# One padding tile on the right side of SBUF grows by 128 bytes, so that large matmul operands begin at multiples of 256 bytes

## The chip, the cores and the metric

The kernel runs on one core of a Trainium2 chip. The metric is the device time of one execution in microseconds (us). SBUF, the on-chip memory that TensorE (PE) reads its operands from, is addressed in bytes within each of its 128 partitions. Pools of tiles are laid out from both of its ends: most pools grow upward from the low end ("left"), pools with `side="right"` grow downward from the high end.

## The reference

One layer of a diffusion backbone over 1024 latent tokens with a prefix of 256 context tokens, D = 1024, all in float32:

```python
h_x = rms_norm(x, g_norm1) * (1 + sc1) + sh1                    # and h_c from the context
y_x, _ = token_mixer(h_x, h_c, ...)   # one input projection h @ w_in, then two branches:
    # A: gelu, layer norm, 128x128 mixing of positions per channel group, @ w_branch_a
    # B: gated linear attention in both directions, in chunks of 64 tokens, @ w_branch_b
    # (sigmoid gate * A + sigmoid gate * B) @ w_out
x = x + gt1 * y_x
tokens = rms_norm(x, g_norm2) * (1 + sc2) + sh2
y = moe_ffn(tokens, ...)              # 16 experts, top group, top 2 in it:
    # (silu(t @ w_g[e]) * (t @ w_u[e])) @ w_d[e], weighted by the router
return rms_norm(x + gt2 * y, g_final)
```

## The kernel before

Every large product is made from float32r operands that are split in two, a high part and the rest: `hi` is a copy on ScalarE (ACT) into float32r, `lo` the difference on VectorE (DVE). A product is then the sum of hi·hi, hi·lo and lo·hi. A matmul has a stationary operand, which an LDWEIGHTS (PEld in the profile) puts into the array, and a moving operand of up to 512 columns, which streams through. In a name such as `mm<-zh,wh` the moving operand stands first and the stationary one second.

The stages that matter here, in the order of time, with the two operands of their matmuls:

- To about 360 us: the rows are normalised into `hxh`, `hxl` (left side), and the projections q, v and k are made. `wload` (line 244) brings 1 MB of a weight into `wraw` and `split` (lines 237 and 238) makes `wh`, `wl` of it; all of these lie on the right side, in pool `wp`. `gemm` (line 256) issues the matmuls. With 512 columns `hx` moves and `w` is stationary; with 256 or 264 columns `w` moves and `hx` is stationary.
- 360 to 686 us: the gated linear attention, and between its blocks further projections (`side_tile`) with `hx` moving over 512 columns.
- 686 to 868 us: the spatial gating, first with `w` moving over 256 columns, then with `hx` moving over 512.
- 868 to 955 us: `@ w_branch_a`, with `zh`, `zl` moving (right side, pool `zp`) and `wh`, `wl` stationary.
- 955 to 1045 us: `@ w_branch_b`, with `gbh`, `gbl` moving (left side) and `wh`, `wl` stationary.
- 1045 to 1153 us: `@ w_out` (line 994), 256 columns: stationary is `m` (right side), moving are `wh`, `wl` (right) for half of the columns and `woh`, `wol` (left) for the other half. The router runs along with it.
- From 1160 us: the experts. A page is 1 MB of an expert's weights. It lands in one of ten page tiles on the right side (`praw`, `raw`), ACT and DVE split it into an `hl` tile (`part`, lines 1192 and 1193), and `block_a` (line 1372) streams the `hl` tile in twelve matmuls of 512 columns past `xah`, `xal`, `aah` or `aal` (left side, stationary). Nine of the experts have further rows, which `block_b` (line 1385) takes straight from the page tile over 256 columns.

Three `hl` tiles take turns. The first two of each round lie in pool `mt1` on the right side, the third in pool `ep` on the left:

```python
def split_tile():
    n = used[1] % 3
    used[1] += 1
    return (ep_ if n == 2 else mt1).tile([128, 2, 2048], F32R, name="hl", tag=("m0", "m1", "hl")[n], bufs=1)

def block_a(acc, st, k0, pg, start, stop):
    wh, wl = pg
    for k in range(2):
        for n, (x, w) in enumerate(((0, wh), (0, wl), (1, wh))):
            for h in range(2):
                end = PE.matmul(acc[h], st[x][:, k0 + k, :], w[:, k, 512 * h:512 * h + 512], ...)
```

One page is thus four matmuls on the stationary `xah`, two on `xal`, four on `xah` and two on `xal`. The engines take their instructions in the order of the program; SyncE (SP) issues nearly all loads of weights, and a load waits until its tile is free.

Two padding tiles stand at the start of the memory: `pad_l` of 16 floats in the left pool `cp`, and `pad_r` of 24 floats, the first tile of the first right pool. Nothing reads them.

Of the kernel before, what the change touches and what calls it, by code (L numbers as in the profile page):

```python
# [6 lines left out]
F32 = mybir.dt.float32  # L7
# [154 lines left out]
def body(tc, A, out):  # L162
# [40 lines left out]

    cp.tile([128, 16], F32, name="pad_l")
    rp = tc.alloc_tile_pool(name="rp", bufs=1, side="right")
    rp.tile([128, 24], F32, name="pad_r")

    def bcast(key, r0, n, tile_, eng=None):
        a = A["rows"]
# [1477 lines left out]
```

## Time and profile before

| | |
|---|---|
| median of 3 runs | 2250.44 us (2249.14 to 3596.91) |
| the profiled execution | 2251.51 us |
| its span, first to last instruction | 2249.8 us |
| mean granted TensorE clock | 0.984 |
| PE busy | 2170.6 us, 96% |
| DVE busy | 1415.1 us, 63% |
| ACT busy | 1056.9 us, 47% |
| DMA | 529.63 MB, mean 235 GB/s |

The time of the execution is 1.7 us longer than its span. Busy time of PE is the union of its matmuls, each from its start to a modelled end; matmuls overlap, so a new one starts well before the one before it ends, and the pace of PE is read from the starts.

### The profile page before, as it was taken

The numbers are of one execution on the slowest core, as the hardware profiler recorded it, in microseconds if no ns is written. First come the engines' busy times: TensorE is split into PE (matmuls) and PEld (weight loads), VectorE is DVE, ScalarE is ACT, GpSimd is POOL, SyncE is SP. The second block draws the span as 40 slices with busy tenths as digits, with TensorE's granted clock in tenths as the row PEclk, the third lists the DMA queues.
The fourth block names the chain that finished last, engine by engine and source line by source line (L and its number), as shares of the span: only waits on it lengthen the run. The fifth ranks groups of instructions, "written<-read, shape, count | busy, mean of one in ns | idle before, by whom it ended". The sixth has DMA issues, their size and how long they took to land. (4 is left out here: it accounts for less than half of the span.)

```text
span 2249.8 us, 36046 instructions
## 1 busy us (share of the span) xinstructions
PE 2170.6 (96%) x14286; PEld 1787.4 (79%) x14287; DVE 1415.1 (63%) x2127; ACT 1056.9 (47%) x1327; POOL 213.0 (9%) x174
## 2 busy tenths in 40 slices
PE   8999999999999999999969999999999999999975
PEld 6999898888889978888967777777778777777754
DVE  5744215847672354245888578787878787677666
ACT  3412114634542244233226456665667576555553
POOL 0011000000000000000342110000101010100031
PEclk9999999999999999999989999999999999999987
DMA  7576433556652176445658779797989898877774
GB/s 295 178 228 177 155 130 102 192 172 208 215 187 71 57 260 208 168 149 195 189 189 319 253 274 362 284 369 297 367 291 377 298 351 314 296 274 284 280 245 157
DMA packets 141792, 529.63 MB, mean 235 GB/s; under 512 B 17127, under 2 KB 57759, under 8 KB 94513
## 3 DMA queue, kind: packets, MB, share of 16 engines
q1 hardware_dynamic: 119584, 467.84, 57.1%
q0 software_dynamic: 20880, 55.16, 8.5%
q10 hardware_dynamic: 1152, 4.26, 0.6%
q8 instruction: 114, 1.87, 0.3%
q14 instruction: 62, 0.50, 0.1%
HBM read 457.09 MB, written 70.31 MB: 234 GB/s over the span
## 5 line engine op out<-in xcount | busy, mean ns | idle before, releaser
L1193 DVE TENSOR_TENSOR hl<-praw,hl 128x2048 fp32r<-128x2048 f32 x174 | 400.2, 2302 | 137.3 <-ACT hl L1192 134.1
L1372 PE MATMUL pa<-hl,xah 128*128 128x512 f32 x1536 | 428.1, 399 | 19.8 <-ACT hl L1192 13.2
L1192 ACT ACTIVATE hl<-praw 128x2048 fp32r<-128x2048 f32 x174 | 333.4, 1918 | 157.8 <-PE pa L1372 150.9
L1372 PEld LDWEIGHTS pa<-hl,xah 128*128 128x128 f32 x1536 | 286.9, 189 | 91.4 <-ACT hl L1192 13.7
L1193 DVE TENSOR_TENSOR hl<-raw,hl 128x2048 fp32r<-128x2048 f32 x114 | 260.7, 2290 | 91.0 <-ACT hl L1192 88.2
L1192 ACT ACTIVATE hl<-raw 128x2048 fp32r<-128x2048 f32 x114 | 218.6, 1918 | 104.0 <-PE pa L1372 98.2
L1372 PE MATMUL pa<-hl,xal 128*128 128x512 f32 x768 | 241.8, 396 | 0.0
L1372 PE MATMUL pa<-hl,aah 128*128 128x512 f32 x768 | 214.8, 401 | 6.3 <-DVE hl L1193 5.0
L256 PE MATMUL mm<-wh,hxh 128*128 128x256 f32 (+1 forms) x768 | 218.2, 284 | 0.9 <-DVE vv L285 0.6
L256 PE MATMUL mm<-wl,hxh 128*128 128x256 f32 (+1 forms) x768 | 216.8, 282 | 0.0
L256 PE MATMUL mm<-wh,hxl 128*128 128x256 f32 (+1 forms) x768 | 216.6, 282 | 0.0
L256 PE MATMUL mm<-hxh,wh 128*128 128x512 f32 x448 | 178.4, 398 | 0.0
L256 PE MATMUL mm<-hxh,wl 128*128 128x512 f32 x448 | 178.2, 398 | 0.0
L256 PE MATMUL mm<-hxl,wh 128*128 128x512 f32 x448 | 178.1, 398 | 0.0
L1372 PEld LDWEIGHTS pa<-hl,xal 128*128 128x128 f32 x768 | 145.5, 189 | 34.0
L1372 PEld LDWEIGHTS pa<-hl,aah 128*128 128x128 f32 x768 | 142.7, 190 | 37.3 <-DVE hl L1193 5.5
L256 PEld LDWEIGHTS mm<-wh,hxh 128*128 128x128 f32 x768 | 144.6, 188 | 1.9 <-DVE vv L285 0.8
L238 DVE TENSOR_TENSOR wl<-wraw,wh 128x2048 fp32r<-128x2048 f32 (+1 forms) x36 | 82.7, 2298 | 99.7 <-ACT wh L237 99.6
L256 PEld LDWEIGHTS mm<-wl,hxh 128*128 128x128 f32 x768 | 144.7, 188 | 0.0
L256 PEld LDWEIGHTS mm<-wh,hxl 128*128 128x128 f32 x768 | 144.4, 188 | 0.0
L1372 PE MATMUL pa<-hl,aal 128*128 128x512 f32 x384 | 121.4, 396 | 0.0
L237 ACT ACTIVATE wh<-wraw 128x2048 fp32r<-128x2048 f32 (+1 forms) x36 | 69.1, 1918 | 67.3 <-PE mm L256 67.0
(489 smaller groups left out, 3588.2 us busy)
## 6 DMA issues: line engine op xcount, KB each, us to landing
praw<-in_w_gu_dram SPq DMA_DIRECT2D x116, 1024.0 KB
raw<-in_w_gu_dram SPq DMA_DIRECT2D x76, 1024.0 KB
praw<-in_w_d_dram SPq DMA_DIRECT2D x58, 1024.0 KB
raw<-in_w_d_dram SPq DMA_DIRECT2D x38, 1024.0 KB
wraw<-in_w_in_dram SPq DMA_DIRECT2D x24, 1024.0 KB
wraw<-in_w_mod_dram SPq DMA_DIRECT2D x18, 1024.0 KB
vb<-v_d POOLq DMA_DIRECT2D x16, 1024.0 KB, 6.3
xt<-in_x_dram SPq DMA_DIRECT2D x16, 512.0 KB
```

The lines of the kernel that those rows point to most:

```text
L237: SC.activation(wh[:, :n], raw[:, :n], AF.Copy)
L238: V.tensor_sub(wl[:, :n], raw[:, :n], wh[:, :n].bitcast(F32))
L256: end = PE.matmul(acc, Wst[a](k), Wmv[b](k), start=n == 0, stop=n == tot - 1)
L1192: SC.activation(hl[:, 0, :], raw, AF.Copy)
L1193: V.tensor_sub(hl[:, 1, :], raw, hl[:, 0, :].bitcast(F32))
L1372: end = PE.matmul(acc[h], st[x][:, k0 + k, :], w[:, k, 512 * h:512 * h + 512], start=start and (k, n) == (0, 0), stop=stop and (k, n) == ( ...
```

## The change

`pad_r` has 56 floats instead of 24: 224 bytes per partition instead of 96.

```diff
     cp.tile([128, 16], F32, name="pad_l")
     rp = tc.alloc_tile_pool(name="rp", bufs=1, side="right")
-    rp.tile([128, 24], F32, name="pad_r")
+    rp.tile([128, 56], F32, name="pad_r")
```

All tiles of right-side pools move down by 128 bytes; those of left-side pools stay. The built programs have these start addresses, as their remainder on division by 256 (their phase, from here on):

| tiles | side | before | after |
|---|---|---|---|
| `wraw`, `wh`, `wl`, and the page tiles `praw`, `raw` | right | 128 | 0 |
| `zh`, `zl`; `m`; the first two `hl` of a round | right | 128 | 0 |
| `S`, `la`, `kb`, `qb`, `vb`, `vg`, `ug` | right | 128 | 0 |
| `xt` at the start; `w2` | right | 32; 96 | 160; 224 |
| `hxh`, `hxl`, `hc`, `gbh`, `gbl`, `woh`, `wol` | left | 0 | 0 |
| `xah`, `xal`, `aah`, `aal`, `xbT`, `abT`, the third `hl` | left | 0 | 0 |
| `kt`, `ats`, `qq` of the attention | left | 64 | 64 |
| `kf` (the identity of the transposes) | left | 128 | 128 |

A slice that a matmul takes of these tiles begins a multiple of 512 bytes further on, with three exceptions: the chunks of 264 columns (1056 bytes apart, so that the slices go through all eight phases of 32 bytes), the 32-column slices of `xbT` and `abT` (128 bytes apart), and the slices of `qq`. Modulo 512 the two buffers of `wh` lie at 384 and 128 before, since one is 8448 bytes long.

The instructions stand in the same order on every engine, and there are as many. Seven instructions wait for other semaphores, because a tile that was moved by 128 bytes overlaps other tiles of pools released earlier. On SP, at the start of the attention over latent tokens, where `mk` is a small mask and `kb`, `qb` are the first loads of the attention:

```order
 L595 DMA r_d<-vs 128x256 [waits DMAHW7_49,Activation_49]
 L607 DMA w2m<-in_kg_dram 128x1 [waits DMAHW0_49,PE_49]
-L750 DMA mk<-in_ki_dram 128x128 [waits DMAHW1_49,DMASW1_49,PE_49]
+L750 DMA mk<-in_ki_dram 128x128 [waits DMASW1_49,DMASW0_49,DMAHW1_49,PE_49,Pool_49]
 L775 DMA kb<-kT_d 128x4x128 [waits DMAHW2_49]
 L776 DMA qb<-qT_d 128x4x128 [waits DMAHW3_49]
```

The load of `mk` now also waits for an instruction of GpSimd and a DMA of its queue: those of `fold_router` (lines 546, 554 and 555), whose tile `wra` it now overlaps. The other six are a wait that is dropped (the first splits of `w2` on ACT, two passes of `la`, and the loads of `rb` and `wra`) or one added for a DMA of GpSimd's queue (one split into `m` on ACT, at about 1000 us; the last such DMAs before it load `vb` in the attention).

## Rows read from the trace of the kernel before

**Rows 1.** The page's first part: busy us (share of the span) and instructions.

```profile
PE 2170.6 (96%) x14286; PEld 1787.4 (79%) x14287; DVE 1415.1 (63%) x2127; ACT 1056.9 (47%) x1327; POOL 213.0 (9%) x174
```

**Rows 2.** What PE waited for: us in total, times, longest us.

```profile
PE pa L1372 <- ACT hl L1192: 14.5, 2, 13.2
PE pa L1372 <- DVE hl L1193: 10.6, 6, 5.0
```

**Rows 3.** Windows in the `zh` and `gbh` stages: PE busy (matmuls), PEclk, DMA, GB/s.

```profile
870.00:950.00 80.00, 80.00 (x355) 1.00 0.62 214
960.00:1040.00 80.00, 80.00 (x345) 1.00 0.46 145
```

**Rows 4.** `zh` and `gbh`: duration ns min/median/max (modelled ends), first and last start.

```profile
L256 PE MATMUL mm<-zh,wh x128: 389/389/395, 868.6 to 955.0; 128*128 128x512 f32 x128
L256 PE MATMUL mm<-gbh,wh x128: 392/394/398, 955.7 to 1044.5; 128*128 128x512 f32 x128
```

**Rows 5.** Timeline of PE where `hx` moves: start us, us, engine, line, operation.

```profile
779.62 0.39 PE L256 MATMUL mm<-hxh,wl 128*128 128x512 f32 x1
...
781.94 0.39 PE L256 MATMUL mm<-hxh,wh 128*128 128x512 f32 x1
```

**Rows 6.** Timeline of PE in the experts: the first matmuls of consecutive pages.

```profile
1691.20 1.08 PE L1372 MATMUL pa<-hl,aah 128*128 128x512 f32 x4
...
1693.93 1.09 PE L1372 MATMUL pa<-hl,xah 128*128 128x512 f32 x4
...
1696.72 1.10 PE L1372 MATMUL pa<-hl,xah 128*128 128x512 f32 x4
...
1699.53 1.08 PE L1372 MATMUL pa<-hl,xah 128*128 128x512 f32 x4
...
1702.26 0.62 PE L1372 MATMUL pa<-hl,xah 128*128 128x512 f32 x2
```

**Rows 7.** The same earlier: the first matmuls of two consecutive pages.

```profile
1511.61 1.09 PE L1372 MATMUL pa<-hl,xah 128*128 128x512 f32 x4
...
1514.38 0.40 PE L1372 MATMUL pa<-hl,xah 128*128 128x512 f32 x1
```

**Rows 8.** ACT's splits of pages alone: how many began before 1691 us.

```profile
1160.00:1691.00 531.00, 278.05 (x145) 0.98 0.83 307
```

**Rows 9.** Timeline of ACT: splits, idle time before them, what ended it.

```profile
1691.40 1.92 ACT L1192 ACTIVATE hl<-raw 128x2048 fp32r<-128x2048 f32 x1 [0.88 <-PE pa L1372]
1694.13 1.92 ACT L1192 ACTIVATE hl<-praw 128x2048 fp32r<-128x2048 f32 x1 [0.81 <-PE pa L1372]
```

**Rows 10.** Groups of matmuls, shapes apart: count, busy us, mean ns (modelled ends).

```profile
L256 PE MATMUL mm<-hxh,wh 128*128 128x512 f32 x448 | 178.4, 398 | 0.0
L256 PE MATMUL mm<-wh,hxh 128*128 128x256 f32 x512 | 144.7, 283 | 0.0
L994 PE MATMUL mm<-woh,m 128*128 128x256 f32 x256 | 49.2, 286 | 0.0
L994 PE MATMUL mm<-wh,m 128*128 128x256 f32 x256 | 49.2, 285 | 0.0
L697 PE MATMUL s<-vb,kt 128*128 128x256 f32 x192 | 31.1, 292 | 0.3
L697 PE MATMUL s<-ctx_v,kt 128*128 128x256 f32 x48 | 7.8, 292 | 0.0
```

**Rows 11.** What SP's page loads waited for: us in total, times, longest.

```profile
SPq L1179 <- DVE hl L1193: 636.9, 198, 21.3
```

**Rows 12.** Splits, 1400 to 2000 us: count, busy us, mean ns, idle before.

```profile
L1193 DVE TENSOR_TENSOR hl<-praw,hl 128x2048 fp32r<-128x2048 f32 x103 | 235.9, 2292 | 82.6 <-ACT hl L1192 80.4 <-DMA praw<-in_w_gu_dram 0.5
L1192 ACT ACTIVATE hl<-praw 128x2048 fp32r<-128x2048 f32 x103 | 197.7, 1919 | 93.6 <-PE pa L1372 93.6
```

**Rows 13.** `fold_router`'s last DMA and the load of `mk`: duration ns, start us.

```profile
L555 POOL DMA_DIRECT2D wr_d<-br x1: 543/543/543, 317.0 to 317.0; - x1
L750 SPq DMA_DIRECT2D mk<-in_ki_dram x1: 394/394/394, 362.4 to 362.4; - x1
```

## Prediction

> **What bounds the kernel now.** I read the page's first part, then what PE waited for, then the pace of PE's matmuls stage by stage, and last the queues that feed it. PE is busy for 96% of the span [rows 1], and its longest waits for the splits are 14.5 and 10.6 us in all, most of it in one wait of 13.2 us [rows 2]. The time is therefore the number of matmuls times the step from one start to the next, and a change that moves no instruction can pay only if it moves that step.
>
> The step differs between stages that do the same thing. In 80 us of the `zh` stage 355 matmuls lie, in 80 us of the `gbh` stage 345 [rows 3]. About two of either number only reach into the window from before, since a record of 389 or 394 ns [rows 4] is longer than a step; so the steps are 80 / 353 = 226.6 ns and 80 / 343 = 233.2 ns. Shape (512 columns), stationary operands (`wh`, `wl`) and granted clock (1.00, the 2.4 GHz level) are the same, and the faster window has the more DMA traffic (0.62 against 0.46). What differs is where the moving operand begins: `zh` in the phase of `wh` (128 and 128), `gbh` not (0 and 128). `hx` over 512 columns is also in another phase than `wh`: ten steps take 781.94 - 779.62 = 2.32 us, 232 ns each [rows 5].
>
> The experts repeat this inside one stage, over one set of stationary tiles in phase 0. Pages begin at 1691.20, 1693.93, 1696.72, 1699.53 and 1702.26 us, so they last 2.73, 2.79, 2.81 and 2.73 us: a short one in each round of three [rows 6]. Which tile that is follows from the splits. 145 of them began before 1691 us [rows 8], so the one at 1691.40 is the 146th and the one at 1694.13 the 147th, the third of its round, into the left `hl`; it starts 0.2 us after PE has left the page that began at 1691.20 [rows 6, 9], which was thus the left tile's. The tile in phase 0 is the fast one here; in the `zh` stage it was phase 128 on both sides. So what counts, as far as these rows go, is that the moving and the stationary operand begin in the same phase. Region is no rival: the first two `hl` lie within the memory that `zh` had. Nor does a distance of 256 bytes hurt: one of the two `wh` buffers is 256 off `zh` modulo 512, the other 0, and the records of `zh` against `wh` lie between 389 and 395 ns, half of them at 389 [rows 4].
>
> **The change part by part.** It costs no instruction. It brings every large pair into phase 0. Right with right (`zh` and `wh`, `m` and `wh`) was equal and stays equal. The terms:
>
> - `gbh`, `gbl`: three products of 128 matmuls [rows 4] are 384, each from 233.2 to 226.6 ns: 384 x 6.6 = 2.5 us.
> - `hx` over 512 columns: 3 groups of 448 [rows 10] and the 96 of q at the start (8 slices, 4 outputs, 3 products), 1440 in all, from 232 to 226.6 ns: 1440 x 5.4 = 7.8 us. None of PE's longest waits is in these stretches, so all of it lies on the path. Upper end, by the `gbh` difference of 6.6: 9.5 us.
> - Experts: 16 experts of 18 pages are 288, of which 192 lie in the right tiles. They go from 2.80 (the mean of 2.79 and 2.81) to 2.73 us by the rows above. Rounding and another row make this less: a left page on `xah` lasted 1514.38 - 1511.61 = 2.77 us [rows 7]. I take 0.065 us, since 0.07 is also what twelve matmuls at 5.4 to 6.6 ns give (0.065 to 0.079): 192 x 0.065 = 12.5 us. Ends: 0.02 us a page (3.8 us) and 0.079 (15.2 us), with 2 us more if the left pages lose their 2.77 as well (half of 96 by 0.04).
> - Matmuls of 256 columns whose operands come into the same phase: 1536 with `w` moving over `hx`, 288 with `hx` or `hc` moving, 384 with `wo` moving over `m`, together 2208. Their mean is 283 ns where phases differ (`wh,hxh`) and 285 where they are the same (`wh,m`); but `woh,m`, which differs too and lies beside the latter, has 286 [rows 10]. So at 256 columns nothing is gained, and from -1 to +2.3 ns is possible; I take +1: 2.2 us lost, between 2.2 gained and 5.1 lost.
> - The 264-column chunks go through all eight phases before and after: 0. The same holds for `block_b`, whose stationary slices alternate between phases 0 and 128, so that the pairs that match and those that don't change places: 0.
> - The attention's `vb` against `kt` goes from a distance of 64 to one of 192. `ctx_v` against `kt` has 192 already, and both show 292 ns [rows 10]: 0. `ats` has the phase of `kt`: 0.
> - ACT and DVE read and write the moved tiles as well. Their splits into right and left tiles share means of 1919 and 2292 ns, and ACT had 93.6 us of idle time before 103 of them [rows 12], which covers some ns each: 0. The page loads end at another phase too, and they wait for tiles anyway [rows 11]: 0.
> - The wait that `mk` gains: `fold_router`'s last DMA was issued at 317.0, the load of `mk` at 362.4 us [rows 13]. Queued behind it on SP are `kb` and `qb`, for which the attention would wait; with 45 us between them the price is 0. The other six edits wait for less or for what has long landed: 0.
>
> Sum: 2.5 + 7.8 + 12.5 - 2.2 = 20.6 us. Against the profiled execution's own 2251.5 us this is 2230.9; against the median of the runs, 2250.4, it is 2229.8. I predict **2230 us**. With the low ends (2.5 + 7.8 + 3.8 - 5.1 = 9.0) it is 2242, with the high ones (2.5 + 9.5 + 17.2 + 2.2 = 31.4) 2220.
>
> Is PE still what is late in the experts? SP's loads of pages waited 636.9 us for tiles to come free [rows 11], so loads run ahead of PE. DVE needs 2.29 us for a page, ACT 1.92 [rows 12]; split, split and page are 1.92 + 2.29 + 2.73 = 6.94 us, and three tiles turn round in 3 x 2.73 = 8.19. Cover remains, 1.2 us a round; if it went, a page would wait for its split.
>
> The Trainium skill speaks against this change: "SBUF — State Buffer", section "Who interferes with whom", gives TensorE two independent read ports, one for the moving operand and one for the weights, and says that it never waits on anyone. By that the phases of two operands can't matter, and the sum would be 0. The trace disagrees: 226.6 against 233.2 ns.
>
> **The rivals.**
>
> *The experts' gain is lost to supply.* A shorter page asks for weights at 1 MB in 2.73 us, and pages wait for DMA, ACT or DVE instead. For it: the DMA share was 0.83 from 1160 to 1691 us, with 307 GB/s [rows 8], and the 1.2 us of cover hold only while ACT and DVE do nothing else. Against it: the loads wait for tiles, not the reverse [rows 11], and ACT's idle time before splits ended with PE [rows 12]. Only the other terms remain: 2251.5 - 2.5 - 7.8 + 2.2 = 2243.
>
> *No gain.* The step is set by something that goes with the stage and the tile but not with phase, or PE's two streams don't meet. For it: no row shows a pair of 0 and 0 with `w` stationary. Against it: the three-page rhythm inside one stage. 2251 us. The page of the Trainium skill named above would have this case.
>
> *Slower.* At 256 columns the weight load of the next matmul has half the time to hide, and equal phases make it collide: 2.3 ns on each of 2208, 5.1 us, mostly in the projections with `w` moving. This decides the sign once the 512-column terms together are under 5.1 us: with none of them 2251.5 + 5.1 = 2257. For it only 285 against 283 ns; against it `woh,m` at 286.
>
> *More than forecast.* Other pairs (the float32 matmuls of the attention, whose phases no row separates) gain as well: below 2220.
>
> **How the numbers follow.** My forecast has a chance of 0.71, the loss to supply 0.12, no gain 0.10, slower 0.03, more than forecast 0.04. The range must take in the forecast's ends, 2220 and 2242, and the loss to supply at 2243: 2220 to 2244, which leaves out 0.17. A measurement of this kernel can tell about 2% from no change, here 45 us. Faster than 2205 would take twice my sum: 0.03. Slower than 2295 has no mechanism with such a price: 0.01. The rest, 0.96, lies within 2%, most of it faster.
>
> **What would show it.** In the profile after, 80 us of the `gbh` stage should hold 355 matmuls, not 345, and the `gbh` and `hxh` groups of 512 columns a mean of 389 ns, as `zh` has. All A-only pages should last about 2.73 us, with no rhythm of three. The groups of 256 columns should stay within 2 ns, and PE's waits for `hl` should not grow beyond the 25 us of now. I am wrong if the `zh` stage slows down (then phase 128 itself was the fast one), if the rhythm of three is still there (then it was the tile, not its phase), or if pages speed up and the span does not (then supply is late).

## The result

| | before | after |
|---|---|---|
| median | 2250.71 us (6 runs, 2249.14 to 3596.91) | 2234.06 us (6 runs, 2232.93 to 2237.04) |
| ratio, with its 95% interval | | 0.9919 [0.9906, 0.9933] |
| profiled execution; its span | 2251.51; 2249.8 us | 2234.38; 2232.6 us |

The run of 3596.91 us was disturbed and is in no comparison. The forecast was 2230 us with a range of 2220 to 2244: the sign and the range hold, and the gain is 17.2 us of span where the sum said 20.6.

The page's first part after: PE has lost 18.6 us of its busy time [rows 1], the other engines nothing.

```profile
PE 2152.0 (96%) x14286; PEld 1788.1 (80%) x14287; DVE 1414.7 (63%) x2127; ACT 1057.8 (47%) x1327; POOL 212.6 (10%) x174
```

What PE waited for, after (us in total, times, longest): the waits for the splits are what they were [rows 2], 25.4 us against 25.1.

```profile
PE pa L1372 <- ACT hl L1192: 14.9, 2, 13.4
PE pa L1372 <- DVE hl L1193: 10.5, 7, 5.0
```

Windows after (PE busy, matmuls, PEclk, DMA share, GB/s): the first lies where `w` moves over 256 columns, the second in the `zh`, the third in the `gbh` stage.

```profile
690.00:760.00 70.00, 70.00 (x586) 1.00 0.16 53
870.00:950.00 80.00, 80.00 (x355) 1.00 0.62 214
960.00:1040.00 80.00, 80.00 (x355) 1.00 0.48 153
```

The `gbh` window has come from 345 to the 355 of the `zh` window, which has not moved [rows 3]. At 256 columns it has gone the other way: the same window of the kernel before held some more.

```profile
690.00:760.00 70.00, 70.00 (x592) 1.00 0.16 54
```

Tiles after (duration ns min/median/max, first and last start): the `gbh` records now read as those of `zh` [rows 4].

```profile
L256 PE MATMUL mm<-zh,wh x128: 389/389/389, 867.1 to 953.5; 128*128 128x512 f32 x128
L256 PE MATMUL mm<-gbh,wh x128: 389/389/389, 954.2 to 1040.5; 128*128 128x512 f32 x128
L256 PE MATMUL mm<-gbh,wl x128: 389/389/389, 954.6 to 1041.0; 128*128 128x512 f32 x128
L1372 PE MATMUL pa<-hl,xah x1536: 387/389/794, 1177.0 to 2188.5; 128*128 128x512 f32 x192
L1372 PE MATMUL pa<-hl,aal x384: 387/389/628, 1215.8 to 2214.6; 128*128 128x512 f32 x192
```

The same three groups before, for their first and last starts:

```profile
L256 PE MATMUL mm<-gbh,wl x128: 392/395/398, 956.1 to 1045.0; 128*128 128x512 f32 x128
L1372 PE MATMUL pa<-hl,xah x1536: 387/393/792, 1180.8 to 2205.7; 128*128 128x512 f32 x192
L1372 PE MATMUL pa<-hl,aal x384: 387/392/628, 1219.6 to 2231.8; 128*128 128x512 f32 x192
```

With the first starts of `gbh`, 955.7 before [rows 4] and 954.2 after, these give the account of the span. Ahead of `gbh` 1.5 us came; the `gbh` stage went from 89.3 to 86.8 us, 2.5; `w_out` and the router from 135.8 to 136.0, -0.2; the experts from 1051.0 to 1037.6, 13.4. The tail is 18.0 us in both. Together 17.2 us.

Timeline of PE in the experts after: three times a page's twelve matmuls, the last of them ahead of a transpose, take 2.72, 2.72 and 2.73 us. The rhythm of three [rows 6] is gone.

```profile
1689.70 1.07 PE L1372 MATMUL pa<-hl,xah 128*128 128x512 f32 x4
...
1692.42 1.07 PE L1372 MATMUL pa<-hl,xah 128*128 128x512 f32 x4
...
1695.14 1.07 PE L1372 MATMUL pa<-hl,xah 128*128 128x512 f32 x4
...
1697.87 0.60 PE L1562 MATMUL aat<-kf,sa 128*128 128x128 f32 x4
```

Timeline of PE after where `hx` moves in a short run between the attention's small matmuls (the first two rows below bound nine steps: 2.08 us) and in a long run (the last two bound ten: 2.26 us, before 2.32 [rows 5]).

```profile
433.29 0.39 PE L256 MATMUL mm<-hxl,wh 128*128 128x512 f32 x1
...
435.37 0.39 PE L256 MATMUL mm<-hxl,wh 128*128 128x512 f32 x1
...
778.24 0.39 PE L256 MATMUL mm<-hxh,wl 128*128 128x512 f32 x1
...
780.50 0.39 PE L256 MATMUL mm<-hxh,wh 128*128 128x512 f32 x1
```

The same short run before took 2.10 us, so 226 ns a step were reached in the long run, 231 in the short one, where it had been 233:

```profile
433.63 0.39 PE L256 MATMUL mm<-hxl,wh 128*128 128x512 f32 x1
...
435.73 0.40 PE L256 MATMUL mm<-hxl,wh 128*128 128x512 f32 x1
```

Groups after (count, busy us, mean ns), answering to [rows 10]:

```profile
L256 PE MATMUL mm<-hxh,wh 128*128 128x512 f32 x448 | 176.4, 394 | 0.0
L256 PE MATMUL mm<-wh,hxh 128*128 128x256 f32 x512 | 145.5, 284 | 0.0
L994 PE MATMUL mm<-woh,m 128*128 128x256 f32 x256 | 49.5, 288 | 0.0
L697 PE MATMUL s<-vb,kt 128*128 128x256 f32 x192 | 31.2, 292 | 0.3 <-DVE at L678 0.2 <-ACT la L632 0.2
```

`hxh` stops at 394 ns, half way to the 389 that I had named as its sign; the groups of 256 columns keep within the 2 ns that I gave them. `vb` against `kt`, moved from a distance of 64 to 192, shows its 292 ns as before.

### The profile page after: what moved, and what is told of

Same layout as the page of the kernel before. It is cut to its first block, busy times and chain, and to the rows that moved or that the text cites. A ratio compares the mean times of both kernels' runs of the same rounds, so it can differ in the third digit from the quotient of the medians.

```text
span 2232.6 us, 36046 instructions
## 1 busy us (share of the span) xinstructions
PE 2152.0 (96%) x14286; PEld 1788.1 (80%) x14287; DVE 1414.7 (63%) x2127; ACT 1057.8 (47%) x1327; POOL 212.6 (10%) x174
## 5 line engine op out<-in xcount | busy, mean ns | idle before, releaser
L1372 PE MATMUL pa<-hl,xah 128*128 128x512 f32 x1536 | 421.1, 395 | 19.8 <-ACT hl L1192 13.4
```

## The experiments

The theory: a matmul of 512 columns has the short step when moving and stationary operand begin in the same phase, and the change pays through that alone. Rivals: that 256-byte multiples are good by themselves; that the region or the tile counts; that any unequal phase costs the same, or less the nearer it is; that some finer multiple, 512, gives more. In what follows a distance is moving minus stationary start, modulo 256, and a step is the mean from start to start in the trace, switches and waits apart.

### Both sides at 128

```diff
-    cp.tile([128, 16], F32, name="pad_l")
+    cp.tile([128, 48], F32, name="pad_l")
```

> The left pad grows by 128 bytes instead of the right one: every large operand on both sides begins at phase 128 (modulo 256), none at a multiple of 256. Equal phases (my theory): as fast as the changed kernel, about 2234 us; 80 us of the gbh stage hold 355 matmuls, and pages of A rows last 2.73 us in all three hl tiles. Rival, that multiples of 256 are what counts: nothing gained, 2251 us or more, 345 matmuls in the gbh stage, and the left hl tile, which leaves phase 0, becomes slow (2.80 us).

2236.31 us (2230.88 to 2237.95), ratio 0.9918 [0.9902, 0.9934]. Its windows in the `zh` and `gbh` stages:

```profile
870.00:950.00 80.00, 80.00 (x355) 1.00 0.63 214
960.00:1040.00 80.00, 80.00 (x355) 1.00 0.46 147
```

The whole gain is there with no large tile on a multiple of 256. What the change is called is not what it works by: the equal phase is.

### Left at 128, right at 0

```diff
-    cp.tile([128, 16], F32, name="pad_l")
+    cp.tile([128, 48], F32, name="pad_l")
...
-    rp.tile([128, 24], F32, name="pad_r")
+    rp.tile([128, 56], F32, name="pad_r")
```

> Both pads grow: the right side is at phase 0 as in the changed kernel, the left side at 128. Equal phases: left and right differ again, so 2249 to 2252 us, 345 matmuls in 80 us of the gbh stage, right hl tiles 2.80 us a page and the left one 2.73. Rival, that the moving operand must begin at a multiple of 256: the right hl tiles stay at 2.73 and the left one goes to 2.80, about 2240 us. Rival, that the phase of the weights counts alone: gbh and hx over 512 columns stay fast (wh is at 0), about 2245.

2255.57 us (2248.98 to 2261.31), 1.0013 [1.0002, 1.0024]. The right side stands as in the changed kernel, and nothing of the gain is left. Its windows in the same two stages:

```profile
870.00:950.00 80.00, 80.00 (x355) 1.00 0.62 214
960.00:1040.00 80.00, 80.00 (x345) 1.00 0.45 144
```

and its timeline in the experts:

```profile
1691.67 1.09 PE L1372 MATMUL pa<-hl,xah 128*128 128x512 f32 x4
...
1694.46 1.10 PE L1372 MATMUL pa<-hl,xah 128*128 128x512 f32 x4
...
1697.26 1.08 PE L1372 MATMUL pa<-hl,xah 128*128 128x512 f32 x4
...
1700.00 1.09 PE L1372 MATMUL pa<-hl,xah 128*128 128x512 f32 x4
```

The slow `gbh` window is back. Two right pages take 2.79 and 2.80 us, the one of the left tile from 1697.26 on 2.74: the rhythm is back too. The theory holds where the rival of multiples falls. Neither operand's phase counts by itself either: `wh` lies at a multiple of 256 and `gbh` is slow, the right `hl` move from one and are slow, the left `hl` move from phase 128 and are fast.

### The experts' tiles alone

```diff
+    pm = tc.alloc_tile_pool(name="pm", bufs=1, side="right")
+    pm.tile([128, 32], F32, name="pad_m")
...
+    pm.release()
```

The pad lies ahead of `m`, the page tiles and the first two `hl`; all else stays as before.

> The kernel before with 128 bytes of padding only ahead of the pools from w_out on, so that m, the right hl tiles and raw go to phase 0, and all before (hx, gbh, wh, zh) stays as it was. The experts' term stands alone: my sum gave it 12.5 us (2238.5 us); the changed kernel's trace has 13.2 us less between its first and last matmul of the experts than the one before, which gives 2238. Rival, supply (the changed kernel's experts gained only since their loads began earlier): under 5 us, 2246 or more. Up to 1045 us the trace should be that of the kernel before: 345 matmuls in 80 us of the gbh stage.

2238.81 us (2236.53 to 2241.75), 0.9936 [0.992, 0.9951]; its span of 2236.6 us is 13.2 below that of before. Windows, then the timeline:

```profile
870.00:950.00 80.00, 80.00 (x354) 1.00 0.62 214
960.00:1040.00 80.00, 80.00 (x345) 1.00 0.45 144
```

```profile
1691.19 1.07 PE L1374 MATMUL pa<-hl,xah 128*128 128x512 f32 x4
...
1693.91 1.07 PE L1374 MATMUL pa<-hl,xah 128*128 128x512 f32 x4
...
1696.63 1.07 PE L1374 MATMUL pa<-hl,xah 128*128 128x512 f32 x4
```

`gbh` is slow, pages take 2.72 us, and the experts' term is there in full. The rival that supply would eat it falls.

### Other distances

Four sizes of `pad_r`, 32 floats as here, 40, 48 and 120, put the right side at 96, 64, 32 and at 0 modulo 512:

```diff
-    rp.tile([128, 24], F32, name="pad_r")
+    rp.tile([128, 32], F32, name="pad_r")
```

> pad_r of 32 floats: the right side at phase 96, left at 0. If every unequal phase costs the same: as the kernel before, 2251 us, gbh step 233 ns (345 matmuls in 80 us). If the cost falls with the distance: between 2251 and 2234, step between 233 and 226.6.

> pad_r of 40 floats: the right side at phase 64, the one that kt and ats of the attention have. If every unequal phase costs the same: 2251 us, gbh step 233 ns. If the period were 64 bytes: as the changed kernel, 2234 us, 226.6 ns. If the cost falls with the distance: about half, 2243 us, 230 ns.

> pad_r of 48 floats: the right side at phase 32, the smallest distance that the tiles can have. If every unequal phase costs the same: 2251 us, 233 ns. If the cost falls with the distance: about 2238 us, 228 ns.

> pad_r of 120 floats: phase 0 as in the changed kernel, but the right side now also begins at multiples of 512 like the left one (the changed kernel: 256 beyond one). If the period is 256 or less: as the changed kernel, 2234 us, 226.6 ns. Rival, that 512 gives a better match still: below 2230, a step under 226.

| right side at | median, us | ratio | `gb` step (distance) | `hl` right step (distance) |
|---|---|---|---|---|
| 96 | 2259.29 | 1.0028 [1.0016, 1.004] | 234.3 (-96) | 233.8 (+96) |
| 64 | 2245.3 | 0.9961 [0.9942, 0.9979] | 233.3 (-64) | 229.6 (+64) |
| 32 | 2252.57 | 1.0003 [0.9991, 1.0015] | 233.3 (-32) | 233.3 (+32) |
| 0 modulo 512 | 2234.69 | 0.992 [0.9903, 0.9937] | 226.7 (0) | 227.6 (0) |

The window of the `gbh` stage at 96, and at 0 modulo 512:

```profile
960.00:1040.00 80.00, 80.00 (x343) 1.00 0.44 145
```

```profile
960.00:1040.00 80.00, 80.00 (x355) 1.00 0.47 153
```

512 gives no more than 256. But two ideas of mine fell: unequal phases don't all cost the same (in the experts +64 costs 2.0 ns over the 227.6 of equal phases, +32 costs 5.7), and the cost doesn't fall as the distance does. At 64 it also has a sign, unless the two stages differ for another reason: +64 in the experts was cheap, -64 in the `gbh` stage dear. The next run exchanges the two.

### Left at 64, right at 0

```diff
-    cp.tile([128, 16], F32, name="pad_l")
+    cp.tile([128, 32], F32, name="pad_l")
...
-    rp.tile([128, 24], F32, name="pad_r")
+    rp.tile([128, 56], F32, name="pad_r")
```

> The changed kernel with pad_l of 32 floats: the left side at phase 64, the right one at 0, the mirror image of the run with the right side at 64. There a moving operand 64 past the stationary one took 229.6 ns (hl), one 64 short of it 233.3 (gbh). If the signed distance decides: now gbh is 64 past wh, near 229.6 ns a step (350 matmuls in 80 us of its stage), and the right hl are 64 short, 233 ns; about 2249 us. Rival, that it was the stage: gbh 233 and hl 229.6 again, about 2245 us.

2248.1 us (2245.96 to 2253.15), 0.9983 [0.9974, 0.9992]. Its window in the `gbh` stage:

```profile
960.00:1030.00 70.00, 70.00 (x308) 1.00 0.45 143
```

Two records reach into it, so the step is 70 / 306 = 228.8 ns, at +64; right `hl`, now at -64, take 233.3. In these two stages the sign goes with the operands and not with the stage.

It is not the whole rule. `hx` over 512 columns is here at +64 too, and ran in two ways; the first two rows below bound 24 steps, and so do the last two:

```profile
775.17 0.40 PE L256 MATMUL mm<-hxl,wh 128*128 128x512 f32 x1
...
780.77 0.40 PE L256 MATMUL mm<-hxl,wh 128*128 128x512 f32 x1
...
845.37 0.39 PE L256 MATMUL mm<-hxl,wh 128*128 128x512 f32 x1
...
850.86 0.39 PE L256 MATMUL mm<-hxl,wh 128*128 128x512 f32 x1
```

That is 5.60 and 5.49 us, 233.3 and 228.8 ns a step. Of the 18 unbroken runs of 15 or more such steps in this kernel ten had the short step and eight the long one. At -64, in the kernel with the right side at 64, all 18 had 233.3 or 233.4. So +64 can be cheap and need not be; no run here shows what decides it.

### The matmuls of 256 columns moved apart

The equal phase costs something at 256 columns. Three kernels keep the change and let the moving operands of `w_out`, and `wh`, `wl` of the two projections that move `w` over 256 columns, begin 128, 32 and 192 bytes further on:

```diff
-    def split(raw, n, k, hi_pool, tag="w"):
-        wh = hi_pool.tile([128, WMAX], F32R, name="wh", tag="wh", bufs=2)
+    def split(raw, n, k, hi_pool, tag="w", o=0):
+        wh = hi_pool.tile([128, WMAX], F32R, name="wh", tag="wh", bufs=2)[:, o:]
...
-        return wload(A["w_in"][:, o:o + 8 * n], 8 * n, 8)
+        return wload(A["w_in"][:, o:o + 8 * n], 8 * n, 8, 32 if name in "rs" else 0)
...
+            if j == 2:
+                t1.tile([128, 32], F32, name="pad_w")
```

(`wl` likewise, and the two splits of `w_out` that go into `wh`, `wl`; 8 and 48 floats instead of 32 in the other two.)

> The changed kernel, with wh, wl of the r and s projections and of w_out begun 128 bytes further into their tiles, and woh, wol 128 bytes higher: all matmuls of 256 columns with w or wo moving have differing phases again, those of 512 columns equal ones. In the changed kernel's trace a step of 256 columns takes 120.0 ns where phases are equal, in the one before 118.65 where they differ. If phase does that: 2304 steps less 0.9 to 1.35 ns, 2.6 us, about 2231.5 us, and 768 matmuls of the s projection 1 us sooner done. Rival, that the 1.3 ns come from something else: 2234, steps stay at 120.

> The changed kernel, with the moving operands of 256 columns (wh, wl of r, s and w_out; woh, wol) begun 32 bytes past phase 0 in place of 128. With the right side at phase 32 such a step took 116.8 ns, at 128 118.65, at equal phases 120.0. If that carries over: 1536 steps less 3.2 ns and 768 less some 2 to 3, about 7 us under the changed kernel, 2227 us. Rival, that the shorter step belonged to that kernel as a whole: 2234.

> The same with 192 bytes past phase 0. Where hc moved at 192 against wh a step of 256 columns took 114.05 ns, where hx did 115.7, where wo did against m 116.8. If the distance from stationary to moving operand decides: 2304 steps less 3 to 6 ns, 7 to 13 us under the changed kernel, 2221 to 2227 us. Rival, that 114 is peculiar to hc and hx moving: a step of 116.8 or more, 2227 or above.

> The changed kernel itself, beside the three others: 0.992 of the kernel before, 2234 us.

| kernel | median, us | ratio to before |
|---|---|---|
| the changed kernel again | 2233.04 (2231.89 to 2237.02) | 0.9913 [0.9899, 0.9927] |
| moved by 128 | 2234.56 (2231.54 to 2237.23) | 0.9917 [0.9902, 0.9932] |
| moved by 32 | 2229.38 (2225.13 to 2232.11) | 0.9894 [0.9876, 0.9912] |
| moved by 192 | 2224.69 (2224.2 to 2226.36) | 0.9875 [0.986, 0.9891] |

The kernel moved by 128 ran beside another set of runs than the other three, so its ratio is the figure to compare. The window where `w` moves over 256 columns, moved by 128, by 32, and by 192:

```profile
690.00:760.00 70.00, 70.00 (x593) 1.00 0.17 59
```

```profile
690.00:760.00 70.00, 70.00 (x602) 1.00 0.15 52
```

```profile
690.00:760.00 70.00, 70.00 (x620) 1.00 0.14 47
```

Two records reach in from before, so the steps are 70/591 = 118.4, 70/600 = 116.7 and 70/618 = 113.3 ns, against 70/584 = 119.9 after. By 128 the price of the change at 256 columns is undone, as the step shows; 2 us of total can't be told from the changed kernel's spread. By 32 the two long stretches with `w` moving took 5.0 us less than in the changed kernel, and the median is 3.7 us lower, where some 7 had been expected. By 192 the same stretches went from 94.4 and 92.1 us to 89.5 and 87.0, 10.1 us together, and the median is 8.4 us under that of the changed kernel on the same chip, with ranges that don't meet. This kernel is faster than the one before and the changed one.

## Why the prediction was right, and where a term was not

**The bound.** PE's steps set the time: its waits for the splits stayed, its step fell, and the span fell with it. That it pays when the moving and the stationary operand begin in the same phase was argued from three stages; two kernels, with the left side at 128 and the right one at 128 or 0, now show it. "No gain" is out. With it falls the reading that the starts of two operands can't matter, which rested on what the Trainium skill says in "SBUF — State Buffer", section "Who interferes with whom", of two independent read ports and of a TensorE that never waits on anyone: with only the starts of its two operands changed, the step of one stage was 226.7, 228.9, 233.3 or 234.3 ns. Whether it is at those ports that the two meet, no run shows.

**`gbh`, 2.5 us.** Measured 2.5, with the 355 matmuls that were named.

**The experts, 12.5 us.** Measured 13.4. The right pages carried the term: their step fell from 232.7 to 227.6 ns, and 192 x 12 x 5.1 is 11.8 us, 0.061 a page where I took 0.065. The left pages gave the rest, which I had put only into the upper end: 229.2 to 227.5 ns, 96 x 12 x 1.7 = 2.0 us.

**256 columns, -2.2 us.** The two long stretches lengthened from 93.4 to 94.4 and from 91.1 to 92.1 us, 2.0 together, and `w_out` with the router by 0.2. That the sum was met to the tenth is luck: the +1 ns was picked between -1 and +2.3, from rows that disagreed, and the step measured 1.3 more (118.7 to 120.0 ns).

**`hx` over 512 columns, 7.8 us.** This term was mis-sized by 4.6 us, more than the whole difference of 3.4 us between sum and span. It came to 3.2. Each line is the time from the first start to the last in both traces (for k, of its four runs):

| where | matmuls | before, us | after, us | gained | forecast |
|---|---|---|---|---|---|
| q, at the start | 96 | 36.42 | 36.37 | 0.05 | 0.5 |
| k, four runs of 48 | 192 | 43.75 | 42.72 | 1.03 | 1.0 |
| between the attention's blocks | 864 | 324.68 | 322.64 | 2.04 | 4.7 |
| spatial gating | 288 | 90.59 | 90.51 | 0.08 | 1.6 |

Two steps of the prediction failed here: that all of this term lies on the path because none of PE's *longest* waits is in these stretches, and that 232 to 226.6 ns, from ten steps of one long run, holds for all 1440.

The path first. Both traces hold the same 14286 matmuls in the same order, so they can be compared start by start. In the attention the steps from one `hx` matmul to the next gained 3.3 us, and all other steps took 1.3 back. In the gating it is 1.3 gained and 1.3 taken back. Together 2.5 of the missing 4.6 us are thus lost outside the steps that got shorter. In the attention they are mostly waits of PE for DVE and ACT. The list for 361 to 686 us has 0.6 us before:

```profile
PE keT L660 <- DVE ke L657: 0.6, 2, 0.3
```

and 1.7 after, with two more of 0.2:

```profile
PE keT L660 <- DVE ke L657: 0.6, 2, 0.3
PE o L686 <- ACT op L763: 0.4, 1, 0.4
PE gate L629 <- DVE w L611: 0.3, 1, 0.3
```

Here a wait does take the place of a part of the time removed, and that recurs: in the seven traces with equal phases at 512 columns these other steps of the attention took 139.3 to 139.9 us, against 138.1 before. (Of the six other kernels with unequal phases three have 138.1 or 138.2, and three 138.9 to 141.0.) The gating is another matter. In 777 to 868 us PE's `mix` had waited 2.7 us for a load and 0.5 for DVE before. After:

```profile
PE mix L872 <- DVE z L874: 2.3, 2, 1.3
PE mix L872 <- DMA vg<-vh_d: 1.6, 3, 0.9
```

That is 0.7 us more in this trace, but 1.3 less than before in the trace of the second run of the changed kernel. The steps of `hx` gained their 1.3 us in the gating in all seven traces, while its other steps took 25.8 to 27.7 us, against 26.4 before; so the 0.08 of the table is chance.

Then the step. In long runs the mechanism held, k gaining all it should. In a run between other matmuls the short step needs time to set in. By place in its run, `hx` had before 231.8 (the first three), 232.3, 233.2 and 231.7 ns (the tenth to twelfth), after 232.1, 229.8, 227.5 and 226.8, and 226.7 from there on. Most runs in the attention end before that: of 188 steps in the first places 76 are left in the tenth to twelfth. This costs about 0.9 us: the 764 steps in the attention that directly follow one another would have gained 4.1 at 5.4 ns each. The left pages of the experts show the same in the kernel before, where each comes behind a page of unequal phases: by threes their steps are 232.3, 228.6, 228.7 and 227.2 ns, and after, behind equal phases, 227.7, 227.5, 227.6 and 227.1. So it isn't the attention's small matmuls alone that delay it; why it is delayed, no run here tested. The last 1.1 us belong to q, whose matmuls stand among others, and to the steps at the ends of runs.

**What was costed at nothing.** Around these terms the account closes: -2.0 for 256 columns and 3.2 for `hx` leave 0.3 of the 1.5 us ahead of `gbh`. That is 0.3 gained in the 264-column chunks (119.67 to 119.35 us), 0.2 gained before 25 us, and 0.2 lost between q and those chunks. The load of `mk` was issued at 362.1 us, 0.3 earlier than before, and the waits for the splits are the same.

**The rivals.** Supply: fell, by the experts' tiles alone. Slower at 256 columns: equal phases are slower there, at less than half of the rival's price, which has nowhere near the weight to decide the sign; whether the weight load is what is held up, as that rival had it, no run shows. More than forecast: not in this kernel, and the one pair of the attention that I followed, `vb` against `kt`, stayed at 292 ns. The version with the 256-column operands moved by 192 gets below the forecast, to 2224.7 us, by another edit.

## What to carry to other kernels

Where TensorE is busy for most of the span, read its step by stage, from the starts: two stages of the same shape with different steps can show more than the list of its waits, as they did here. Then compare where the two operands of each pair begin, moving against stationary, and set padding so that pairs of 512 float32r columns match. At 256 columns matched pairs were among the slowest here, so try the distances; the best one wasn't the nearest. Size such a gain by the length of the runs in which these matmuls stand, since the short step came in full only in long ones, and look for short waits right behind them: a gain on PE is kept only as far as what it does next is ready.

## What the runs showed of the hardware

For float32r matmuls with a weight load for each (14287 loads for 14286 matmuls on the page); steps in ns by distance, moving minus stationary modulo 256. They are means over unbroken runs, from the tenth step on, nearly all of them in the stages from 205 to 1045 us at a granted clock of 1.00; the rest are those of `w_out`. The steps of `hl` are means over all of the experts, where the granted clock was 1.00 from 1300 to 2100 us and about 0.9 on either side.

| columns | 0 | +32 | +64 | +96 | 128 | -96 | -64 | -32 |
|---|---|---|---|---|---|---|---|---|
| 512 | 226.7 | | 228.8 or 233.3 | | 231.7 to 233.5 | 234.2 to 234.6 | 233.3 | 233.3 |
| 512, right `hl` | 227.6 | 233.3 | 229.6 | 233.8 | 232.7 | | 233.3 | |
| 256 | 120.0 | 116.7 to 117.8 | 113.3 or 117.8 | 120.0 | 118.0 to 120.0 | 117.3 to 119.3 | 113.3 or 117.8 | 118.3 to 118.6 |

What is best at 512 columns is among the worst at 256. At 64 the distance alone doesn't settle the step. At 512 columns `hx` at +64 had both values in one kernel. At 256 columns, in the kernel with the left side at 64, `w` over `hx` at -64 ran at 113.3 ns in the stretch to 360 us and at 117.8 in the one from 682 us, over the same pairs of phases, while the one moved by 192 had 113.3 in both. What chooses between the two, and what in the memory or the array makes a distance dear, these runs leave open; so they do whether the weight load or the stream is the one that is held up.
